# Splitting the SSD layer's weights by transfers: a cast on the way in, and a second, accumulating transfer for the remainder

## The chip, the cores and the metric

The kernel runs on one core of one Trainium2 chip. The metric is the device time of one execution in microseconds, given as the median of several runs. The profile and the trace come from one more execution of the same program.

## The reference, cut to what matters

One inference step through two layers, in float32: a Mamba-2 SSD mixer and then a gated MLP with position mixing, each behind an RMS norm and added to the residual. 640 tokens (512 of a new stream, 8 times 16 of running streams) of width 1024 go through. The change touches the weights of the first layer's two projections:

```python
def mamba2_mixer(h, conv_prev, ssm_prev, w_in, conv_w, conv_b, dt_bias, a_log, d_skip, norm_w, w_out):
    proj = h @ w_in
    z = proj[..., :D_INNER]
    xbc = proj[..., D_INNER:D_INNER + CONV_DIM]
    dt_raw = proj[..., D_INNER + CONV_DIM:]
    xbc_c, conv_new = causal_dwconv(xbc, conv_prev, conv_w, conv_b)
    xbc_c = jax.nn.silu(xbc_c)
    ...
    y, ssm_new = ssd_scan(xs, dt, a, bm, cm, ssm_prev)
    y = y + d_skip.astype(jnp.float32)[:, None] * xs.astype(jnp.float32)
    y = gated_group_rms_norm(y.reshape(bsz, seq_len, D_INNER), z, norm_w).astype(h.dtype)
    return y @ w_out, conv_new, ssm_new.astype(ssm_prev.dtype)
```

## The kernel before

Matrix products run on values in the type float32r, which keeps fewer bits than float32. To hold the accuracy, each operand is split into a high part H (the value rounded to float32r) and a low part L (what is missing), and a product is three matmuls: H by H, H by L and L by H. Activations are split when they are made. The weights come from memory as float32 tiles of 128 x 1024 (512 KB) and are split on the core.

The split of the first layer's weights is `wsplit` (L93). SP issues the transfer into a tile `raw` (L95; two buffers), ScalarE copies it into `wh` with the rounding (L99), and VectorE or POOL subtracts: `wl` = `raw` - `wh` (L100). Both `wh` and `wl` have four buffers. `Stream` (L106) keeps the list of tiles in order of use; `next` hands out the next tile and first calls `wsplit` for tiles up to two beyond it (`Stream(units, 2)`, L318). `on_pool` (L317) names the tiles whose subtraction is on POOL: tiles 3 to 6, all tiles z0 and all tiles of the output projection; the others are on VectorE. The very first tile goes another way (`first`, L116) and isn't touched by the change.

The work goes by eight groups of four heads. For a group, the input projection is made of six tiles, x0, x1, B, C, z0 and z1 (those of x0 and x1 of the second group are done within the first; 48 matmuls each in `in_proj`, L258), and from the second group on two tiles "o" of the output projection of the group before. PE's order in a group is: x0, x1, B, C, z0, then scan, output projection of the group before (ten pieces of 512 columns, `out_proj`, L270) and the pair products mixed, then z1. After the last group of this layer the stream's list goes on into tiles of the second layer; what is loaded ahead of these is not used.

Behind each projection of x0, x1, B and C stands a convolution, `conv_tile` (L406). POOL clears and fills the first columns of `xp`, VectorE moves the PSUM result into it, POOL copies the last columns out, ScalarE does the first tap and VectorE the other three, and then ScalarE a tanh:

```python
            G.memset(xp[:, 0:3], 0.0)
            G.tensor_copy(out=xps[:, :, 0:3], in_=cch[:, j])
            V.tensor_tensor(out=xp[:, 3:387], in0=o0, in1=rb[:, 0:384], op=ALU.mult)
            ...
            G.tensor_copy(out=nconv[:, j, 0, :], in_=xp[:, 512:515])
            G.tensor_copy(out=nconv[:, j, 1:9, :], in_=xps[:, :, 16:19])
            ...
            S.activation(acc[:, 0:664], xp[:, 0:664], AF.Identity, scale=cw[:, 4 * ft:4 * ft + 1],
                         bias=cw[:, 128 + ft:129 + ft])
            for k in range(1, 4):
                V.scalar_tensor_tensor(acc[:, 0:664], xp[:, k:k + 664], cw[:, 4 * ft + k:4 * ft + k + 1], acc[:, 0:664],
```

Its result `xc` (L428, L429) is transposed by PE (`to_tokens`, L465) in the middle of the next projections, and from the transposed x VectorE makes `xdt` (L479) and POOL `xw` (L481). Other work of POOL in a group: eight products that decay the old states (`h`, L587) and one mask of `E` (L631). `E` are tiles of decays, read by SP from a table in device memory (`laD`, L513), one per head, and worked on by ScalarE (L515, L516).

PE's instructions run in the order of the code. In this layer the order on the other engines is made when the kernel is built, by a scheduler that places instructions by their estimated times and by what they wait for; every engine then works its list in that order, and an instruction that waits holds up those behind it. DMA issues stand in the list of the engine that issues them. In the second layer all orders are those of the code. Of the first layer's norm, the sum of squares (L185 to L189) and the projection of dt (`dtT`, L182) matter below.

Of the kernel before, what the change touches and what calls it, by code (L numbers as in the profile page):

```python
# [8 lines left out]
F32 = mybir.dt.float32  # L9
F32R = mybir.dt.float32r  # L10
I32 = mybir.dt.int32
AF = mybir.ActivationFunctionType
ALU = mybir.AluOpType
PSUM = bass.MemoryType.PSUM

P = 128
# [24 lines left out]
def hybrid_step(ctx: ExitStack, tc: tile.TileContext, xin, xT0, cst, wdt, cache, wA, wAo, h0in, wB, wBv, wBo,  # L41
                lnwb, spc, bsp, nwb, y_out, nconv_out, sspP_out, sspS_out, v_out):
    nc = tc.nc
    V, S, G, T = nc.vector, nc.scalar, nc.gpsimd, nc.tensor
# [3 lines left out]
    wpool = ctx.enter_context(tc.tile_pool(name="wpool", bufs=3))  # L48
# [13 lines left out]
    def C(n):  # L62
        a, b = _C[n]
        return csb[0][:, a:b] if b <= NCST1 else csb[1][:, a - NCST1:b - NCST1]
# [25 lines left out]
        return r  # L90


    def wsplit(eng, pool, src, scale=None):  # L93
        raw = (pool or wpool).tile([P, 1024], F32, name="raw", tag="raw", bufs=2)
        nc.sync.dma_start(out=raw, in_=src)  # L95
        H = wpool.tile([P, 1024], F32R, name="wh", tag="wh", bufs=4)
        L = wpool.tile([P, 1024], F32R, name="wl", tag="wl", bufs=4)
        if scale is None:
            S.copy(out=H, in_=raw)  # L99
            eng.tensor_tensor(out=L, in0=raw, in1=H.bitcast(F32), op=ALU.subtract)  # L100
        else:
            S.activation(H, raw, AF.Identity, scale=scale)
            V.scalar_tensor_tensor(L, raw, scale, H.bitcast(F32), ALU.mult, ALU.subtract)
        return H, L

    class Stream:  # L106
        def __init__(self, srcs, ahead):
            self.srcs, self.ahead, self.got, self.n, self.pools = srcs, ahead, [], 0, {}

        def fill(self, ahead):  # L110
            while len(self.got) < min(len(self.srcs), self.n + ahead):
                i = len(self.got)
                self.got.append(wsplit(G if i in on_pool else V, self.pools.get(i), *self.srcs[i]))


        def first(self, n, between):  # L116
# [141 lines left out]
    def in_proj(W, xT, pool=None, tag="in", at=(1, 3, 5, 7, 9, 11, 13)):  # L258
        outs = []
        for h, (a, b) in enumerate(HALVES):  # L260
            o = (pool or ps_in).tile([P, 512], F32, name="pin", tag=tag)[:, :b - a]
            outs.append(o)
            for k in range(KD):
                in_proj_step(W, xT, o, h, k)
                if 8 * h + k in at:
                    pump()
        return outs
# [36 lines left out]
    units, names = [], []  # L304
# [9 lines left out]
        units += [p[1:] for p in part]  # L314
    units += wo(GROUPS - 2) + wo(GROUPS - 1)
    units += [(wBv[i],) for i in range(16)]
    on_pool = {3, 4, 5, 6} | {i for i, n in enumerate(names) if n in ("z0","o")}  # L317
    stream = Stream(units, 2)  # L318


    with ExitStack() as ca:
# [35 lines left out]
        for d in (15, 13, 11, 9, 7, 5, 3):  # L357
# [17 lines left out]
                        in1=C("blk").rearrange("p (b o) -> p b o", o=1).broadcast_to([P, 8, HEADS]), op=ALU.mult)  # L375
# [69 lines left out]
        for g in range(GROUPS):  # L445
# [77 lines left out]
            if g:  # L523
                queue(0, *(() if g == 1 else (0,)))
                o = in_proj(stream.next(), xT, ps_m, "m", at=(3, 7, 11, 14))
                xcs.append(conv_tile(*o, 16 + g, 2, *cio))
                queue(1, *(() if g == 1 else (1,)))
                o = in_proj(stream.next(), xT, at=(3, 7, 11, 14))
# [683 lines left out]
```

## Time and profile before

| | us |
|---|---|
| median of 3 runs | 1113.79 |
| lowest, highest | 1112.61, 1121.4 |
| the profiled execution | 1111.67 |
| its span, first to last instruction | 1109.9 |

| engine | busy us | share of the span |
|---|---|---|
| PE (matmuls) | 1035.4 | 93% |
| PEld (weight loads, beside the matmuls) | 931.0 | 84% |
| DVE (VectorE) | 903.4 | 81% |
| ACT (ScalarE) | 442.6 | 40% |
| POOL (GpSimd) | 204.2 | 18% |

The first layer takes the first 620 us or so of the span. "Busy" counts the time in which an engine has at least one instruction at work. A releaser is what an idle engine waited for last. The time from a transfer's issue to its landing is shown with the tile that it fills.

### The profile page before, as it was taken

The page shows a single profiled execution, that of the slowest core. Times are in us where ns is not written, and L with a number is a line of the kernel's source. Part 1 is how long each engine was busy: PE and PEld are TensorE (multiplying, and loading weights), DVE is VectorE, ACT ScalarE, POOL GpSimd, SP SyncE. Part 2 cuts the span into 40 slices and gives each one's busy share as a digit, 9 for nine tenths or more (in the row PEclk, how much of TensorE's full clock was granted, in tenths as well). Part 3 has the DMA queues.
Part 4 walks back from the last instruction along what each step waited for, and adds up shares of the span by engine and source line. Part 5 has one row for each costly group of instructions (what it writes and reads, how often), then busy time and mean ns, then how long its engine had stood idle before and what let it go on. Part 6 is the DMA issues. An engine that isn't in the chain of part 4 may idle for free.

```text
span 1109.9 us, 16925 instructions
## 1 busy us (share of the span) xinstructions
PE 1035.4 (93%) x6387; PEld 931.0 (84%) x6387; DVE 903.4 (81%) x1575; ACT 442.6 (40%) x803; POOL 204.2 (18%) x303
## 2 busy tenths in 40 slices
PE   8898999898999998989999899987999999999996
PEld 7797888798898897987997688877898988988985
DVE  7869887979878888798789866667888888888876
ACT  6363516235163262452532443354433432423343
POOL 3434323404224043042141000000000000000000
PEclk9898999999999999999999899999999999999998
DMA  7453534253363442623533322202322412413222
GB/s 252 137 181 102 166 114 162 88 177 98 93 207 100 122 144 86 208 71 103 202 94 126 131 72 80 84 22 78 95 81 65 131 59 81 135 50 90 89 67 94
DMA packets 57216, 125.93 MB, mean 113 GB/s; under 512 B 9104, under 2 KB 27792, under 8 KB 57136
## 3 DMA queue, kind: packets, MB, share of 16 engines
q1 hardware_dynamic: 57136, 124.87, 35.5%
q8 instruction: 50, 0.82, 0.3%
q14 instruction: 30, 0.25, 0.1%
HBM read 107.98 MB, written 16.86 MB: 112 GB/s over the span
## 4 chain that ended last, share of the span: by engine, by line
PE 42%; DVE 36%; ACT 10%; DMA 6%; issue 4%; SPq 0%; POOL 0%; ACTq 0%; DVEq 0%
PE pop L69 11%; PE pin L69 9%; PE pv L69 7%; DVE acc L422 7%; DMA E<-laD 5%; DVE wf L749 4%; PE pqb L69 3%; PE pqc L69 2%; PE pqa L69 2%; ACT E L515 2%; DVE h L965 2%; DVE E L631 2%; PE st L69 2%; PE yB L69 1%; ACT wf L748 1%
## 5 line engine op out<-in xcount | busy, mean ns | idle before, releaser
L69 PE MATMUL pin<-xH,wh 128*128 128x384 f32 (+1 forms) x768 | 249.1, 324 | 10.9 <-DVE xp L412 10.2
L69 PE MATMUL pin<-xH,wl 128*128 128x384 f32 (+1 forms) x768 | 239.1, 311 | 0.5 <-DVE wl L100 0.5
L69 PE MATMUL pin<-xL,wh 128*128 128x384 f32 (+1 forms) x768 | 238.8, 311 | 0.0
L69 PEld LDWEIGHTS pin<-xH,wh 128*128 128x128 f32 x768 | 146.8, 191 | 19.0 <-ACT xc L428 11.3
L69 PEld LDWEIGHTS pin<-xL,wh 128*128 128x128 f32 x768 | 147.3, 192 | 0.4 <-issue 0.3
L69 PEld LDWEIGHTS pin<-xH,wl 128*128 128x128 f32 x768 | 146.9, 191 | 0.8 <-DVE wl L100 0.8
L422 DVE SCALAR_TENSOR_TENSOR acc<-xp,cw,acc 128x664 f32<-128x664 f32 x96 | 115.8, 1206 | 19.2 <-ACT acc L419 17.9
L69 PE MATMUL pop<-wf,yHL 128*128 128x512 f32 x480 | 116.4, 398 | 8.7 <-DVE h L965 8.0
L69 PEld LDWEIGHTS pop<-wf,yHL 128*128 128x128 f32 x480 | 88.8, 188 | 34.2 <-DVE h L965 12.8
L99 ACT CAST wh<-raw 128x1024 fp32r<-128x1024 f32 x65 | 67.6, 1042 | 102.9 <-PE pin L69 62.6
L749 DVE TENSOR_TENSOR wf<-raw,wf 128x512 fp32r<-128x512 f32 x128 | 88.0, 692 | 25.1 <-ACT wf L748 22.7
L69 PE MATMUL pop<-wh,yHL 128*128 128x512 f32 x320 | 103.5, 405 | 5.2 <-DVE hs L566 4.4
L748 ACT CAST wf<-raw 128x512 fp32r<-128x512 f32 x128 | 76.5, 615 | 78.8 <-PE pop L69 28.8
L69 PEld LDWEIGHTS pop<-wh,yHL 128*128 128x128 f32 x320 | 57.7, 188 | 20.9 <-DVE hs L566 6.7
L686 DVE SCALAR_TENSOR_TENSOR h<-pop,rr,h 128x512 f32<-128x512 f32 x80 | 58.8, 742 | 12.0 <-PE pop L69 11.9
L69 PE MATMUL pqa<-xH,wf 128*128 128x320 f32 x256 | 63.6, 317 | 5.3 <-ACT v L841 3.2
L69 PE MATMUL pqb<-tf,wf 128*128 128x320 f32 x384 | 63.0, 313 | 2.0 <-DVE zz L1027 2.0
L69 PE MATMUL pv<-wh,xL 128*128 128x512 f32 x160 | 63.4, 396 | 1.0 <-DVE xL L231 1.0
L69 PE MATMUL pv<-wh,xH 128*128 128x512 f32 x160 | 63.7, 398 | 0.0
L69 PE MATMUL pv<-wl,xH 128*128 128x512 f32 x160 | 63.3, 395 | 0.0
L69 PE MATMUL pop<-wl,yHL 128*128 128x512 f32 x160 | 62.6, 391 | 0.0
L862 POOL MEMSET spt<- 64x64 f32 x8 | 1.2, 146 | 320.6 <-DMA spt<-spc 184.4
(221 smaller groups left out, 2072.5 us busy)
## 6 DMA issues: line engine op xcount, KB each, us to landing
raw<-wA SPq DMA_DIRECT2D x47, 512.0 KB, 3.8
raw<-wB SPq DMA_DIRECT2D x32, 512.0 KB, 3.8
E<-laD SPq DMA_DIRECT2D x32, 320.0 KB, 6.8
raw<-wBv SPq DMA_DIRECT2D x18, 512.0 KB, 3.8
h<-h0in SPq DMA_DIRECT2D x16, 512.0 KB, 4.7
raw<-wAo SPq DMA_DIRECT2D x16, 512.0 KB, 4.1
out_sspS<-h SPq DMA_DIRECT2D x16, 512.0 KB, 3.7
raw<-wBo SPq DMA_DIRECT2D x16, 512.0 KB, 3.7
```

The costliest lines, as they stand in the source:

```text
L69: T.matmul(out, lhsT=lhsT, rhs=rhs, start=start, stop=stop, **kw)
L99: S.copy(out=H, in_=raw)
L422: V.scalar_tensor_tensor(acc[:, 0:664], xp[:, k:k + 664], cw[:, 4 * ft + k:4 * ft + k + 1], acc[:, 0:664], ALU.mult, ALU.add)
L515: S.activation(E_[:, t, :], E_[:, t, :], AF.Relu, bias=la[:, t, h:h + 1], scale=-1.0)
L631: (G if i and (last or e) else V).tensor_tensor(out=Es[2 * i + e], in0=Es[2 * i + e], in1=CBm, op=ALU.mult)
L686: V.scalar_tensor_tensor(h1[:, t, dsl], ps, rg[:, t:t + 1], h1[:, t, dsl], ALU.mult, ALU.add)
L748: S.copy(out=t[:, 0], in_=src)
L749: V.tensor_tensor(out=t[:, 1], in0=src, in1=t[:, 0].bitcast(F32), op=ALU.subtract)
L862: G.memset(spt[64:128, 0, 0:64], 0.0)
L965: V.scalar_tensor_tensor(h1[:, t, dsl], ps, 0.5, h1[:, t, dsl], ALU.mult, ALU.add)
```

## The change

`wsplit` has no `raw` tile, no subtraction and no choice of engine any more. POOL issues a transfer from the float32 weights into the float32r tile `wh` (the cast transfer, L97 of the changed kernel). ScalarE writes the negated `wh` into `wl` (L98). POOL then issues a second transfer of the same weights, which adds them to what stands in `wl` (the accumulating transfer, L99). `next` calls `wsplit` for tiles up to three beyond the one it hands out, where it was two.

```diff
-    def wsplit(eng, pool, src, scale=None):
-        raw = (pool or wpool).tile([P, 1024], F32, name="raw", tag="raw", bufs=2)
-        nc.sync.dma_start(out=raw, in_=src)
+
+    def wsplit(src):
         H = wpool.tile([P, 1024], F32R, name="wh", tag="wh", bufs=4)
         L = wpool.tile([P, 1024], F32R, name="wl", tag="wl", bufs=4)
-        if scale is None:
-            S.copy(out=H, in_=raw)
-            eng.tensor_tensor(out=L, in0=raw, in1=H.bitcast(F32), op=ALU.subtract)
-        else:
-            S.activation(H, raw, AF.Identity, scale=scale)
-            V.scalar_tensor_tensor(L, raw, scale, H.bitcast(F32), ALU.mult, ALU.subtract)
+        G.dma_start(out=H, in_=src)
+        S.activation(L, H.bitcast(F32), AF.Identity, scale=-1.0)
+        G.dma_start(out=L, in_=src, accum_op=ALU.add)
         return H, L
...
-                self.got.append(wsplit(G if i in on_pool else V, self.pools.get(i), *self.srcs[i]))
+                self.got.append(wsplit(*self.srcs[i]))
...
-    on_pool = {3, 4, 5, 6} | {i for i, n in enumerate(names) if n in ("z0","o")}
-    stream = Stream(units, 2)
+    stream = Stream(units, 3)
```

PE's order is the same but for the numbers of some tiles. The lines of the changed kernel behind the diff carry numbers that are 5 lower: L405 there is L410 here. Three places of the new orders follow.

POOL, from the end of one group's second stretch on, in the kernel before: the subtraction L100 for two tiles, the memset and copy into `xp` (L410, L411), the copies out (L416, L417) and `xw` (L481).

```order
L100 TENSOR_TENSOR wl<-raw,wh 128x1024
L410 MEMSET xp 128x3
L411 COPY xp<-cch 128x8x3
L416 COPY nconv<-xp 128x3
L417 COPY nconv<-xp 128x24
L100 TENSOR_TENSOR wl<-raw,wh 128x1024
L481 TENSOR_TENSOR xw<-xdt,esu 128x4x128
L410 MEMSET xp 128x3
L411 COPY xp<-cch 128x8x3
L481 TENSOR_TENSOR xw<-xdt,esu 128x128
```

The same place on POOL in the changed kernel, where L97 is the cast and L99 the accumulating transfer:

```order
L97 DMA wh<-wA 128x1024
L411 COPY nconv<-xp 128x3
L412 COPY nconv<-xp 128x24
L405 MEMSET xp 128x3
L406 COPY xp<-cch 128x8x3
L99 DMA wl<-wA 128x1024
L97 DMA wh<-wAo 128x1024
L411 COPY nconv<-xp 128x3
L412 COPY nconv<-xp 128x24
L476 TENSOR_TENSOR xw<-xdt,esu 128x4x128
L99 DMA wl<-wAo 128x1024
L476 TENSOR_TENSOR xw<-xdt,esu 128x128
```

Cast and accumulating transfers take turns, tile by tile, with POOL's other work between and behind them; each L99 waits for ScalarE's negation of the tile just cast.

ScalarE at the start of a group in the kernel before: the cast from `raw` (L99), the convolution's first tap (L419) and tanh (L428), and the work on `E`.

```order
L99 CAST wh<-raw 128x1024
L419 ACTIVATE acc<-xp,cw 128x664
L516 ACTIVATE E<-E 128x640
L515 ACTIVATE E<-E,la 128x128 x6
L516 ACTIVATE E<-E 128x640
L515 ACTIVATE E<-E,la 128x128
L428 ACTIVATE xc<-acc 128x512
L428 ACTIVATE xc<-acc 128x128
L515 ACTIVATE E<-E,la 128x128 x4
L99 CAST wh<-raw 128x1024
L419 ACTIVATE acc<-xp,cw 128x664
```

The same place in the changed kernel; L98 is the negation, L414 the first tap, L423 the tanh:

```order
L98 ACTIVATE wl<-wh 128x1024
L675 ACTIVATE y<-y 128x640
L510 ACTIVATE E<-E,la 128x128 x5
L511 ACTIVATE E<-E 128x640
L414 ACTIVATE acc<-xp,cw 128x664
L510 ACTIVATE E<-E,la 128x128 x6
L511 ACTIVATE E<-E 128x640
L98 ACTIVATE wl<-wh 128x1024
L423 ACTIVATE xc<-acc 128x512
L423 ACTIVATE xc<-acc 128x128
```

The weight instruction stood behind the first tile's tanh and now stands ahead of it.

POOL at the start of the program in the kernel before, with the sums of squares on L188:

```order
L410 MEMSET xp 128x3 x2
L188 ISA
L188 TENSOR_TENSOR sqa_125<-sqa_125,xt 128x640 x3
L411 COPY xp<-cch 128x8x3 x2
L100 TENSOR_TENSOR wl<-raw,wh 128x1024 x2
```

And in the changed kernel, where they are on L184:

```order
L405 MEMSET xp 128x3 x2
L97 DMA wh<-wA 128x1024 x3
L99 DMA wl<-wA 128x1024
L184 ISA
L184 TENSOR_TENSOR sqa_125<-sqa_125,xt 128x640
L99 DMA wl<-wA 128x1024
L184 TENSOR_TENSOR sqa_125<-sqa_125,xt 128x640
L99 DMA wl<-wA 128x1024
L184 TENSOR_TENSOR sqa_125<-sqa_125,xt 128x640
L97 DMA wh<-wA 128x1024
```

Three cast transfers are issued at once, and each sum stands behind an accumulating transfer.

## Rows read from the trace of the kernel before

**Rows 1.** The page's part 1: busy us, share of the span, instructions, by engine.

```profile
PE 1035.4 (93%) x6387; PEld 931.0 (84%) x6387; DVE 903.4 (81%) x1575; ACT 442.6 (40%) x803; POOL 204.2 (18%) x303
```

**Rows 2.** Windows: us, busy PE, PEld, DVE, ACT, POOL, clock, DMA share, GB/s: stretches x0-z0.

```profile
313.60:353.70 40.10, 37.53 (x263) 36.51 (x262) 34.42 (x61) 23.52 (x49) 14.63 (x23) 1.00 0.48 150
...
sum 246.50, PE 228.83 PEld 222.41 DVE 206.62 ACT 141.94 POOL 84.03; mean PE 38.14 PEld 37.07 DVE 34.44 ACT 23.66 POOL 14.00
```

**Rows 3.** The same by window: five stretches between those; the start.

```profile
sum 161.90, PE 157.45 PEld 131.63 DVE 137.87 ACT 29.92 POOL 32.50; mean PE 31.49 PEld 26.33 DVE 27.57 ACT 5.98 POOL 6.50
...
0.00:165.90 165.90, 150.04 (x987) 136.81 (x988) 136.99 (x238) 74.84 (x142) 58.02 (x76) 0.96 0.49 159
```

**Rows 4.** Chain of waits, 313 to 347 us: start, us, what.

```profile
313.57 5.04 DMA E<-laD
...
322.66 2.32 DVE acc L422
...
330.34 2.35 DVE rt L85
...
339.80 2.26 DVE acc L422
```

**Rows 5.** Timeline, 329 to 331 us, DVE and POOL: start, us, what.

```profile
330.14 0.17 DVE L84 TENSOR_TENSOR rt<-rr 128x5 f32<-128x5 f32 x1
330.34 2.34 DVE L85 SCALAR_TENSOR_TENSOR rt<-rt,rx 128x5 f32<-128x5 f32 x1
...
330.26 2.40 POOL L100 TENSOR_TENSOR wl<-raw,wh 128x1024 fp32r<-128x1024 f32 x1 [0.37 <-ACT wh L99]
```

**Rows 6.** Tile acc, first 620 us: ns min/median/max, first and last start.

```profile
L422 DVE SCALAR_TENSOR_TENSOR acc<-xp,cw,acc x96: 894/909/2994, 39.7 to 568.8; 128x664 f32<-128x664 f32 x96
```

**Rows 7.** Groups by line, first 620 us: busy us, mean ns | idle before, releasers.

```profile
L99 ACT CAST wh<-raw 128x1024 fp32r<-128x1024 f32 x65 | 67.6, 1042 | 102.9 <-PE pin L69 62.6 <-PE pop L69 34.0 <-DMA raw<-wA 6.3
L100 POOL TENSOR_TENSOR wl<-raw,wh 128x1024 fp32r<-128x1024 f32 x23 | 55.9, 2432 | 13.5 <-ACT wh L99 13.5
L100 DVE TENSOR_TENSOR wl<-raw,wh 128x1024 fp32r<-128x1024 f32 x42 | 52.6, 1252 | 7.1 <-ACT wh L99 7.0
```

**Rows 8.** Tiles raw, then E: issues on SP in ns; landing in us.

```profile
L95 SPq DMA_DIRECT2D raw<-wA x47: 327/334/1452, 8.2 to 537.1; - x47
...
DMA to landing us min/median/max: 3.3/3.8/7.7
...
DMA to landing us min/median/max: 4.1/6.8/9.5
```

**Rows 9.** Timeline, POOL, the long form of xw.

```profile
334.38 1.65 POOL L481 TENSOR_TENSOR xw<-xdt,esu 128x512 f32<-128x512 f32 x1 [1.72 <-DVE xdt L479]
```

**Rows 10.** Windows of 4 us: columns as in rows 2.

```profile
316.00:320.00 4.00, 4.00 (x32) 4.00 (x31) 2.77 (x5) 2.19 (x5) 0.00 (x0) 1.00 0.98 337
```

**Rows 11.** Timeline, ScalarE: tanh of x0.

```profile
327.24 0.83 ACT L428 ACTIVATE xc<-acc 128x512 f32<-128x512 f32 x2 [0.58 <-DVE acc L422]
```

**Rows 12.** Timeline, PE: first matmuls of x0 and x1, transposes, a gap.

```profile
313.12 0.34 PE L69 MATMUL pin<-xH,wh 128*128 128x384 f32 x1
...
320.16 0.34 PE L69 MATMUL pin<-xH,wh 128*128 128x384 f32 x1
...
329.87 0.60 PE L469 MATMUL tp<-csb,xc 128*128 128x128 f32 x4
...
345.90 0.41 PE L69 MATMUL pin<-xH,wh 128*128 128x384 f32 x1 [1.93 <-DVE xp L412]
```

**Rows 13.** Timeline of the start: ScalarE, POOL, DVE.

```profile
19.43 0.72 ACT L182 COPY dtT<-pin 64x384 f32<-64x384 f32 x2
...
18.46 1.73 POOL L188 TENSOR_TENSOR sqa<-sqa,xt 128x640 f32<-128x640 f32 x1 [0.39 <-ACT xt L187]
...
22.86 0.82 DVE L189 TENSOR_TENSOR sqa<-sqa,sqa 128x640 f32<-128x640 f32 x1
```

**Rows 14.** Transfers, first 620 us: packets, MB, share of 16 engines.

```profile
q1 hardware_dynamic: 37199, 86.04, 43.4%
```

More of the change, by code (lines that the diff above doesn't have):

```diff
@@ L107, in __init__ @@
         def __init__(self, srcs, ahead):
-            self.srcs, self.ahead, self.got, self.n, self.pools = srcs, ahead, [], 0, {}
+            self.srcs, self.ahead, self.got, self.n = srcs, ahead, [], 0
         def fill(self, ahead):
```

## The prediction

> **What bounds the kernel now.** I read the page's busy shares first: PE has work in 93% of the span and DVE in 81%, POOL in 18% [rows 1]. PE is near its end, DVE close behind. The change touches only the first 620 us (the SSD layer), so I cut that part by what PE does. From the third group of heads on, each group has two stretches. In the first, five input projections run back to back (x0, x1, B, C, z0): six such stretches take 246.5 us, of which PE is busy 228.83, so 17.7 us are idle, 2.9 us each [rows 2]. In the second, the output projection and z1 run: five of them leave PE idle for 161.9 - 157.45 = 4.5 us, under 1 us each [rows 3]. The first 165.9 us (start, first two groups) leave 15.9 us idle [rows 3]. So whatever VectorE gains, about 18 us can come from the six stretches, and a few more from the start.
>
> What holds PE in a stretch is read from the chain of waits [rows 4]: a transfer of E, the ScalarE work behind it, then for 23 us VectorE with hardly a break, until PE starts again at 345.90 after 1.93 us of idle. Three of these VectorE steps take 2.3 us, and the timeline shows why for one of them: a tile of 128x5 elements, 0.17 us otherwise, takes 2.34 us while POOL does one of the subtractions of wsplit, 2.40 us [rows 5]. The other two are convolution steps on L422, whose median is 0.91 us and whose longest takes 2.99 [rows 6].
>
> **What goes.** wsplit's subtraction leaves both engines: 42 on DVE, 52.6 us, and 23 on POOL, 55.9 us [rows 7], and with these the stalls just shown. In a stretch VectorE is busy 34.4 of 40.1 us [rows 2]. It loses about two subtractions of its own (2.5 us) and, with POOL's three, three stalls of 1.4 to 2.2 us (2.3 less 0.9 or 0.17): some 8 us. It then needs 26 us for 40 and isn't the bound; the 2.9 us of idle would go. I take them in full, 6 x 2.9 = 17.7 us, since the waits named in a stretch are VectorE's or hang on its xc.
>
> **What comes.** ScalarE keeps one instruction per tile: the negation for the cast, 1024 elements each, 1.04 us [rows 7]. Nothing on balance. SP loses its 65 issues, POOL gets two for each of 66 tiles (one more is loaded ahead). Neither a cast nor an accumulating transfer, nor any transfer issued by POOL, stands in the trace, so their cost has to be bounded.
>
> The order on POOL is what matters. A tile is now cast transfer, wait, accumulating transfer, and POOL's next cast transfer stands behind that wait: POOL handles nearly one tile at a time. Before, a transfer of one tile waited for nothing of another but its raw buffer. So each tile has a loop: issue of the accumulating transfer of the tile before, issue and landing of the cast, ScalarE's turn, negation.
> - Issue: on SP one takes 0.33 us [rows 8]. POOL may have to do more; its nearest row of work of its own, one step of the xw product, takes 1.65 [rows 9]. These are my bounds; I take the middle, 1.0.
> - Landing, from issue: 3.8 us median for these tiles, 3.3 to 7.7; E's take 6.8 [rows 8]. With 0.67 more for the issue I take 4.5 as a base. The cast follows an accumulating transfer of the same size on the same queue, issued 1.0 us earlier. At the 337 GB/s of a window with the engines 98% busy [rows 10], 512 KB take 1.56 us; reading source and old contents makes that 3.1, so the cast waits 2.1 us for it at most, 0 at least. I take 1.05: landing 5.5.
> - ScalarE: 1.05 us, and half of one such instruction, 0.5, until it is free.
>
> The loop is 1.0 + 5.5 + 0.5 + 1.05 = 8.05 us; with all lower bounds 0.33 + 3.8 + 1.04 = 5.2, with no queueing 7.0, with the full 2.1 us 9.1, and 10 to 12 if landings go to the upper end of their row.
>
> One of the Trainium skill's rules would make it shorter. It gives transfers issued by POOL as about 2.0 us plus bytes over 436 GB/s (DMA: Bandwidth & Descriptors, "Anatomy of one DMA — SWDGE (gpsimd) path"), 3.2 us for 512 KB. No row of before shows a transfer by POOL; the row of SP's has 3.8. With 3.2 in place of 5.5 the loop would be 5.75 us, less than PE takes for a projection, and the outcome would be that of the fast rival below. Against it, another of its rules says that an engine consumes descriptors in ring order (same page, "Queues, rings and completion order"); by that the cast does stand behind the accumulating transfer, as I assume.
>
> PE's projection takes 7.05 us without a gap (313.12 to 320.16, [rows 12]). Buffers come free one per projection, so in a stretch five loads come at PE's pace and the loop must keep up. The weights themselves aren't late: a buffer freed at 320.16 is needed three projections on, 21 us later, and loop plus a second landing are some 14. What is late is what stands behind the wait. ScalarE's new order puts the negation ahead of the tanh of the convolution (xc, L428), which in before ran at 327.24 [rows 11], and PE transposes that result at 329.87 [rows 12]. Count from the buffer's release at 320.16: landing 5.5, ScalarE 0.5 and 1.05, tanh 0.83, VectorE's xc 0.9 make 328.9: 0.9 us to spare on the first tile. Each further tile is 8.05 - 7.05 = 1.0 us later, and POOL's memset and copy into xp, and the xw product, stand behind the accumulating transfer too. So a stretch changes by 5 x (8.05 - 7.05) - 2.9 = +2.1 us; six make +12.6. The second stretches have two loads in 24 us of output projection and don't change.
>
> At the start POOL has an accumulating transfer ahead of the third sum of squares; that waits for a negation which ScalarE's order puts behind the copies of dtT (19.43 + 0.72 us). 20.15 + 1.05 + 1.0 = 22.2 for a sum that began at 18.46, 1.73 us, and whose result was added at 22.86 [rows 13]: 22.2 + 1.73 = 23.9, 1.1 us late, and up to 3 if the first casts take bandwidth from xt. I take +2. VectorE's relief in the first 165.9 us could give some of its 15.9 us back; the bounds are 0 and 8, and I take 0, since this part also has its loads one after another.
>
> **The sum.** +12.6 + 2 = +14.6 us on a span of 1109.9 us (execution 1111.67). The median of the runs lies 2.1 us higher, at 1113.79: I predict 1128 us.
>
> **The rivals.**
> - *The loop keeps up* (under 7.05 us; no queueing, or transfers by POOL as quick as the skill's fit). Then the six stretches give 17.7 us and the start costs 2: 1098, at best 1090 with the start's 8 us. For it: 3.8 us is the median of SP's transfers, and the loop with no queueing is 7.0. Against it: from 316 to 320 us the DMA engines are 98% busy [rows 10], with the transfers of E (6.8 us, [rows 8]) just where a stretch begins, and accumulating transfers come on top. Chance 0.25.
> - *Both cancel* (loop 7.05 to 7.7 us): 6 x (5 x 0.35 - 2.9) + 2 = -5 at its middle, 1109. Chance 0.16.
> - *The DMA engines become the bound.* They are 43.4% busy over the 620 us [rows 14]; a stretch is at 0.48 of 40.1 us [rows 2], 19.2 us, of which five loads are 7.8. If an accumulating transfer takes three times a plain one (4.7 us), five tiles need 31 us, with the rest 42.5, more than the stretch. E's transfers then land up to three such, 14 us, later; less the 2.9 us, 6 x 11.1 + 2 gives 1182. Nothing in the trace speaks for the factor three, nothing against it. Chance 0.12.
> - *The change doesn't do what it says*: a subtraction left on VectorE. Its new order has none, so no chance.
>
> **Chances and range.** The likeliest case, a loop of 7.7 to 9.2 us, has 0.47 and runs by the same formula from 1118 to 1163. A run of this kernel can be told from no change at about 1% (1102.7 to 1124.9). Faster: the first rival and a little of the second, 0.27. Same: the rest of the second and the lower end of the likeliest, 0.23. Slower: 0.50. The range of 8 in 10 goes from 1094 (the fast rival but for its best part) to 1170.
>
> **What would show it.** POOL's rows of both transfers: their duration, near 1.0 us; the median landing of the cast, near 5.5, and of the accumulating transfer. In a stretch: a time from one cast's issue to the next of 8 us, not 7; waits of ScalarE on the wh transfer and of PE or its weight load on xc, where VectorE's accumulations now take 0.9 us and VectorE is busy about 26 us in 40. The prediction is wrong if casts land within 4.5 us of their release (then PE's idle in a stretch goes below 1 us), or if the accumulating transfers fill the DMA engines (share over 0.9 in the stretches, and PE waiting for wl itself).

## The result, and the profile after

The change makes the kernel slower: 1181.72 us median (1178.22 to 1188.45) against 1115.88 in runs taken beside it, ratio 1.0592, 95% interval [1.0526, 1.0658], or 66 us. The direction was predicted; 1128 us was far too little, and 1182 lies above the range's 1170. The profiled execution took 1181.53 us, its span 1179.4, 69.5 more than before's.

I cut both traces at the same places of the program, at TensorE's first matmul of x0 and last of z0 in each group from the third on. First the kernel before, cut this way, a little wider than in [rows 2, 3]: six first stretches, then five second ones (windows; columns as in rows 2).

```profile
sum 247.66, PE 229.99 PEld 223.67 DVE 206.67 ACT 143.58 POOL 84.03; mean PE 38.33 PEld 37.28 DVE 34.45 ACT 23.93 POOL 14.00
...
sum 158.96, PE 154.51 PEld 128.69 DVE 136.43 ACT 27.39 POOL 32.50; mean PE 30.90 PEld 25.74 DVE 27.29 ACT 5.48 POOL 6.50
```

The same views of the changed kernel, with one stretch of each kind ahead of its sum:

```profile
332.23:377.82 45.59, 39.60 (x266) 38.47 (x265) 26.85 (x54) 22.29 (x44) 12.82 (x29) 0.96 0.70 192
...
sum 271.68, PE 237.66 PEld 229.62 DVE 160.85 ACT 132.28 POOL 76.54; mean PE 39.61 PEld 38.27 DVE 26.81 ACT 22.05 POOL 12.76
...
377.82:416.21 38.39, 32.84 (x207) 27.08 (x206) 24.95 (x44) 7.62 (x12) 11.70 (x16) 0.96 0.58 127
...
sum 185.93, PE 160.85 PEld 132.17 DVE 125.66 ACT 39.23 POOL 58.18; mean PE 32.17 PEld 26.43 DVE 25.13 ACT 7.85 POOL 11.64
```

So the 69.5 us are: first stretches +24.0, second stretches +27.0, the rest of the program from the last z0 on (572.2 to the end, now 625.8 to the end) +16.0, the start +2.6. VectorE did fall to 26.8 us in a stretch, but TensorE's idle time in the first stretches went from 17.7 to 34.0 us. Its busy time grew too, by 7.7 and 6.3 us, with the same matmuls: the granted clock reads 0.96 or less in eight of the eleven stretches, where before it was 1.00 in all but one.

The waits of the first 690 us (who waited for whom: us, times, longest), for POOL, ScalarE, VectorE and TensorE:

```profile
POOL wl L99 <- ACT wl L98: 204.9, 58, 11.8
POOL wh L97 <- PE pop L69: 87.3, 8, 14.2
...
ACT wl L98 <- DMA wh<-wA: 102.2, 32, 9.1
...
DVE CBm L591 <- DMA dhl<-hl: 25.4, 6, 5.6
...
PE tp L464 <- DVE xc L424: 33.9, 14, 4.9
```

The first and third are the loop that the prediction describes, and the last is where it reaches TensorE: these waits for xc lie in the first stretches and are all but 0.1 of the 34.0 us of idle time there. The wait for dhl was not foreseen. POOL's timeline of one first stretch has the casts' issues, and the chain of waits has one turn of the loop:

```profile
332.63 0.55 POOL L97 DMA_DIRECT2D wh<-wA  x1 [3.85 <-PE pin L69]
...
341.47 0.82 POOL L97 DMA_DIRECT2D wh<-wA  x1
...
352.90 0.87 POOL L97 DMA_DIRECT2D wh<-wAo  x1
...
362.29 0.61 POOL L97 DMA_DIRECT2D wh<-wAo  x1
...
371.88 0.61 POOL L97 DMA_DIRECT2D wh<-wA  x1
...
379.49 0.89 POOL L97 DMA_DIRECT2D wh<-wA  x1
```

```profile
352.90 6.34 DMA wh<-wAo
...
359.31 1.07 ACT wl L98
360.38 0.42 issue
360.80 0.89 POOL wl L99
361.70 0.44 POOL xw L476
...
362.29 6.54 DMA wh<-wAo
```

Five turns take 46.9 us, 9.4 each (7.6 to 11.4; the mean over all six stretches is 9.4 too), where 8.05 was predicted and TensorE needs 7.05 for a projection alone.

Behind a first stretch the chain shows a second mechanism. hl holds the samples' xw and B; SP sends it to DRAM as dhl, and it shares its one buffer with CBm, so VectorE may not write CBm until that transfer has landed. ScalarE's negation stands ahead of a tanh, that ahead of VectorE's xc, and behind xc in VectorE's order stands the last piece of hl (L487):

```profile
295.15 1.06 ACT wl L98
296.21 0.53 ACT xc L423
...
296.76 0.89 DVE xc L424 x2
297.66 0.07 DVE hl L487
...
297.89 6.75 DMA dhl<-hl
...
304.73 0.48 DVE CBm L591
...
309.46 2.93 PE pop L69 x6
```

### The profile page after: what moved, and what is told of

It reads as the page before. It is cut to its first block, busy times and chain, and to the rows that moved or that the text cites. A ratio compares the mean times of both kernels' runs of the same rounds, so it can differ in the third digit from the quotient of the medians.

```text
span 1179.4 us, 16944 instructions
## 1 busy us (share of the span) xinstructions
PE 1053.0 (89%) x6387; PEld 945.2 (80%) x6387; DVE 826.2 (70%) x1533; ACT 447.1 (38%) x804; POOL 228.2 (19%) x412
## 4 chain that ended last, share of the span: by engine, by line
PE 29%; DVE 22%; DMA 19%; issue 16%; ACT 8%; POOL 5%; SPq 0%; POOLq 0%; ACTq 0%; DVEq 0%
PE pv L69 9%; DMA wh<-wAo 7%; PE pop L69 6%; PE pin L69 5%; DMA wh<-wA 4%; DVE wf L744 4%; DMA dhl<-hl 3%; PE pqb L69 2%; DMA E<-laD 2%; ACT wl L98 2%; PE pqc L69 2%; DMA out_sspS<-h 2%; POOL wl L99 2%; DVE h L960 2%; PE pqa L69 1%
## 5 line engine op out<-in xcount | busy, mean ns | idle before, releaser
L69 PE MATMUL pin<-xH,wh 128*128 128x384 f32 (+1 forms) x768 | 252.5, 329 | 0.1
L69 PE MATMUL pin<-xL,wh 128*128 128x384 f32 (+1 forms) x768 | 241.8, 315 | 0.0
L69 PE MATMUL pin<-xH,wl 128*128 128x384 f32 (+1 forms) x768 | 241.7, 315 | 0.0
L69 PEld LDWEIGHTS pin<-xH,wh 128*128 128x128 f32 x768 | 149.8, 195 | 7.9 <-issue 4.3
L69 PEld LDWEIGHTS pin<-xL,wh 128*128 128x128 f32 x768 | 149.9, 195 | 0.2
L98 ACT ACTIVATE wl<-wh 128x1024 fp32r<-128x1024 f32 x66 | 69.9, 1059 | 192.0 <-DMA wh<-wA 102.2
L417 DVE SCALAR_TENSOR_TENSOR acc<-xp,cw,acc 128x664 f32<-128x664 f32 x96 | 91.9, 957 | 35.1 <-ACT acc L414 33.5
L424 DVE SCALAR_TENSOR_TENSOR xc<-xc,acc 128x512 f32<-128x512 f32 x64 | 35.5, 594 | 59.4 <-ACT xc L423 59.3
L99 POOL DMA_DIRECT2D wl<-wA x47 | 41.3, 878 | 176.6 <-ACT wl L98 151.5
```

The source lines that it names most:

```text
L69: T.matmul(out, lhsT=lhsT, rhs=rhs, start=start, stop=stop, **kw)
L98: S.activation(L, H.bitcast(F32), AF.Identity, scale=-1.0)
L99: G.dma_start(out=L, in_=src, accum_op=ALU.add)
L424: V.scalar_tensor_tensor(o, o, 1.0, a, ALU.add, ALU.mult)
```

## The experiments

All times are medians, each compared with the kernel before as run on the same chip (1115.4 to 1116.2 us). The table at the end of the section has every run by the four parts of the program.

**Loop or load.** The negation and the accumulating transfer of a tile (wlow) come one tile later, just ahead of the next cast (wcast).

```diff
-self.got.append(wsplit(*self.srcs[i]))
+self.got[i - 1] = wlow(self.got[i - 1], *self.srcs[i - 1])
+self.got.append(wcast(*self.srcs[i]))
```

> Two theories on the 66 us that the change costs. T1, the waits in the orders: POOL's accumulating transfer waits for ScalarE's negation, that for the cast's landing, and all that stands behind on POOL and ScalarE waits too. T2, the load: two transfers of 512 KB for each tile, one of them accumulating, make every transfer land later. This kernel is the changed one with the same transfers, negations and sizes, but with the negation and the accumulating transfer of a tile issued one tile later, just ahead of the next cast, so that the cast has had a projection's time (7 us) to land. T1: ScalarE's wait for the cast, 148 us in the changed kernel, falls below 40 us, the six first stretches go from 48 us back to 42 or less, and the time is 1140 us or lower. T2: the landings stay at 6.5 us, the stretches above 46 us, and the time is over 1165 us.

1176.52 us, ratio 1.0546 [1.0516, 1.0577]. ScalarE still waited 154 us for casts and POOL 204 us for negations. The time lies in T2's range, but this decides nothing: in POOL's order each cast still stands behind the accumulating transfer of the cast before it, so the loop was whole. It was moved, not cut.

**A plain second transfer.**

```diff
-G.dma_start(out=L, in_=src, accum_op=ALU.add)
+G.dma_start(out=L, in_=src)
```

> The changed kernel with the second transfer plain instead of accumulating (the low parts are then the weights themselves: this part of the computation is changed); every instruction and its order stay. T1 (waits in the orders): the loop of cast, negation and second transfer stays, so 1165 to 1182 us. T2 (load, with the accumulation as its dear part): the DMA engines' time on the weights falls by a third or more, the landing of the casts goes from 6.6 towards 4.5 us, and the time is 1145 us or lower.

1130.06 us, 1.0116 [1.0095, 1.0138]: 52 of the 66 us hang on the accumulation. In this kernel casts land in 5.0 us median instead of 6.1 (each follows the second transfer of the tile before on one queue), and POOL's second issue takes 0.53 us instead of 0.88. The first stretches lose 26 us. By the forecast the time speaks for T2, but what changed fits a shorter loop and a lighter load alike.

**The load alone.**

```diff
 nc.sync.dma_start(out=raw, in_=src)
+twin = twins[0].tile([P, 1024], F32, name="twin", tag="twin", bufs=2)
+nc.sync.dma_start(out=twin, in_=src)
```

> The kernel before, with every weight tile from the third on loaded a second time by SP into a tile that nobody reads: the load of the changed kernel without an accumulation and without a wait. T1: landings get later, by 1 to 2 us, but the weights are loaded early enough, 1113 to 1125 us. T2: the transfers of E and of the samples' stack land as late as in the changed kernel (dhl 6.9 us instead of 2.4), and the time is 1135 us or more.

1121.22 us, 1.0041 [1.0025, 1.0058], first stretches 251.2 us, second ones unchanged. Twice the weight traffic from SP's queue costs 5 us, and dhl lands in 3.4 us. T2 as a mere load falls.

**The cast alone.**

```diff
-S.copy(out=H, in_=raw)
+G.dma_start(out=H, in_=src)
```

> One half of the change alone: the high parts come by a cast transfer of POOL, the tile is also loaded as before by SP, and the low parts are subtracted as before on VectorE and POOL; no accumulating transfer, no instruction of ScalarE. T1: POOL's transfers wait only for a free buffer, so the loop is gone: 1105 to 1130 us. T2: two loads of each tile as in the changed kernel, one of them plain: 1140 us or more.

1162.78 us, 1.0423 [1.0398, 1.0448]: in T2's range and a miss for T1 as I had put it. POOL waits 136 + 93 us at the cast's issue, for TensorE to free a wh buffer, and 23 subtractions and the xw products stand behind that; SP in turn waits 134 us for POOL's subtractions before it may load raw again. A wait for a free buffer, harmless on SP, blocks POOL's work.

**The loop cut.** A scheduler sets POOL's order, and it would put the accumulating transfer first again. So both of these kernels hold POOL to the order of the program text. From the third group on, the orders of all engines are the same but for the tile that negation and accumulating transfer handle and one VectorE step on hl in each group.

```diff
+ca.enter_context(tc.manual_schedule(engines={mybir.EngineType.Pool}))
```

> The changed kernel with POOL's instructions of the SSD layer held in the order of the program text, as a control for the next run; in the six first stretches POOL's order is cast, accumulating transfer of the same tile, then the rest, as in the changed kernel. All theories: 1170 to 1190 us.

```diff
-self.got.append(wsplit(*self.srcs[i]))
+self.got.append(wcast(*self.srcs[len(self.got)]))
+self.low(len(self.got) - 2)
```

> The control with one difference: the accumulating transfer (and its negation) in each place is that of the tile cast before, not of the tile cast just ahead of it. The transfers, their number and their order by kind stay; a cast now has a whole projection to land before POOL waits for it. L, the loop: cast, landing, negation and accumulating transfer, one tile at a time, take over 8 us against the 7.05 us of a projection; that the plain second transfer gave back 51 us comes from a loop shorter by 1.6 us, 5 x 6 times. By L ScalarE's wait for casts falls below 50 us, the first stretches from 48 to 43 us or less, and the time is 1145 us or lower. A, the accumulations themselves: they hold the DMA engines so long that the other transfers land late whatever POOL's order is: landings stay as late, the time is 1160 us or more.

1278.09 us, 1.1437 [1.1394, 1.1480], and 1205.92 us, 1.0815 [1.0772, 1.0858]. The control missed by 90 us: in text order POOL's mask products of a pair stand behind casts that wait for the output projection to free its buffers (TensorE waits 63 us for them), and second stretches take 47 us. But the two differ in little else than that one tile, and the first stretches don't have those masks. The control's windows of these, then POOL's wait from the third group on:

```profile
sum 282.91, PE 240.36 PEld 230.15 DVE 174.94 ACT 137.03 POOL 78.10; mean PE 40.06 PEld 38.36 DVE 29.16 ACT 22.84 POOL 13.02
```

```profile
POOL wl L98 <- ACT wl L97: 270.4, 44, 9.9
```

With the loop cut:

```profile
sum 254.81, PE 231.23 PEld 221.26 DVE 154.52 ACT 129.46 POOL 83.80; mean PE 38.54 PEld 36.88 DVE 25.75 ACT 21.58 POOL 13.97
```

```profile
POOL wl L98 <- ACT wl L97: 15.1, 9, 2.3
```

POOL's wait goes from 270 to 15 us and the first stretches lose 28.1 us, though accumulations and transfers are all still there and E lands later (8.8 us, 7.0 in the control). So the loop costs 28.1 / 30 = 0.94 us for each tile in this pair: 19.0 us are idle time of TensorE (0.63 a tile), and 9.1 are its busy time, at a granted clock of 0.93 to 1.00 in the control and 1.00 without the loop. The forecast's other signs of L missed: ScalarE's wait for casts is 113 us there, not under 50, and the time, with a control 90 us off, is far above 1145.

**No cast, no loop.** SP loads, ScalarE rounds and negates, POOL only accumulates; then the same without accum_op, and without the last line.

```diff
-G.dma_start(out=H, in_=src)
+nc.sync.dma_start(out=raw, in_=src)
+S.copy(out=H, in_=raw)
 S.activation(L, H.bitcast(F32), AF.Identity, scale=-1.0)
 G.dma_start(out=L, in_=src, accum_op=ALU.add)
```

> The other half of the change alone: the tile comes by SP into a buffer and ScalarE rounds it into the high parts, as before; ScalarE negates them and POOL's accumulating transfer adds the tile a second time. No cast transfer. L (loop): SP fetches two tiles ahead, so nothing goes round in a loop, POOL waits for ScalarE alone: 1110 to 1140 us. A (accumulations): they are all still there: 1155 us or more.

> The kernel without a loop (SP loads, ScalarE rounds and negates, POOL's second transfer) with that second transfer plain instead of accumulating; every instruction and wait stays in its place (the low parts are then the weights themselves). With the accumulation its six first stretches took 251.2 us, without any second transfer 229.8. If the 21 us are the accumulations' time in the DMA engines (by the queue's busy time 3.1 us for one, 1.75 for a plain one, and E's transfers behind them): stretches of 230 to 238 us, 1110 to 1120 us in all. If they are POOL's instructions behind its wait for ScalarE's negation: 246 us or more, over 1128 us.

> What the relief of VectorE alone can give. SP loads the tile and ScalarE rounds it, as in the kernel before; ScalarE writes the negated high parts, and nothing is added to them (the low parts are left out of the computation): no subtraction, no transfer by POOL, one load for each tile. The prediction's gain: without the subtractions the 17.7 us of idle time in the six first stretches go: these fall from 247.7 to about 231 us, and the time to about 1095 us. Rival: VectorE isn't what ends the wait last, ScalarE's work on E after its transfer is: the first stretches stay above 243 us, the time above 1106 us. Against the kernel with the same work and the accumulating transfer (1136 us) the difference is what 66 such transfers cost without a loop.

1136.07 us, 1.0181 [1.0146, 1.0216]; 1116.60 us, 1.0003 [0.9988, 1.0019]; 1084.55 us, 0.9721 [0.9694, 0.9747]. The first lies in L's range. The last shows the predicted gain in full:

```profile
sum 229.82, PE 227.37 PEld 222.55 DVE 164.73 ACT 171.80 POOL 38.99; mean PE 37.89 PEld 37.09 DVE 27.46 ACT 28.63 POOL 6.50
```

17.8 us less than before in the first stretches, and 9 more at the start. Against it 66 accumulating transfers without a loop cost 51.5 us, and 66 plain ones 32. In the first stretches 21.4 us come with the accumulations, of which making them plain gives back only 7.0; the forecast for that run had 13 or more, or under 5, and neither came. How the other 14 divide between one more load (3.5 us in the run that loaded twice, less than one profile varies by) and POOL's work behind its wait for ScalarE stays open.

From these kernels, one profile each, the first stretches of the changed one add up within rounding: 247.7, less 17.8 for the relief, with 21.4 for the accumulating transfers without a loop and 20.5 for the casts on POOL, which close the loop, make 271.7.

**hl in a buffer of its own**, and then also without the three tiles of wBv that the stream loads at its end and nobody uses.

```diff
-hl = wk.tile([P, 2, 384], F32R, name="hl", tag="CBm", bufs=1)
+hl = wk.tile([P, 2, 384], F32R, name="hl", tag="hl", bufs=1)
```

> The changed kernel with one tile, hl, in a buffer of its own instead of CBm's, the order of all instructions unchanged. In the changed kernel VectorE waits 25 us in all for the transfer of hl to land before it may write CBm, and the second stretches are 12 us longer than before. If this wait is what makes them longer: 1168 to 1175 us, second stretches back to 32 to 33 us. If the wait lies beside another (the loop or the clock), less than 4 us change: 1178 us or more.

```diff
-units += [(wBv[i],) for i in range(16)]
```

> The last kernel with hl in a buffer of its own, and without the tiles of wBv at the end of the stream's list: three of them are loaded, cast, negated and accumulated there though the next layer loads its own. In the kernel with hl's own buffer the time from the last z0 to the end of the program was 551.4 us, against 537.7 before the change. If these tiles are what the border between the layers costs: 538 to 541 us, so 1141 to 1146 us in all. If the border waits for something else: over 1150 us.

> The kernel before, without the tiles of wBv at the end of the stream's list (two are loaded and split there without use). If they cost the border what they take on VectorE and ScalarE, 2 x 1.25 us and some of the transfers: 1110 to 1114 us; if they lie beside other work, 1114 to 1117 us.

1155.05 us, 1.0332 [1.0290, 1.0375], with the order of all instructions unchanged. The second stretches by windows:

```profile
sum 158.51, PE 154.61 PEld 128.65 DVE 125.72 ACT 39.03 POOL 58.35; mean PE 30.92 PEld 25.73 DVE 25.14 ACT 7.81 POOL 11.67
```

All 27 us of them are gone, clock included: the shared buffer was their whole cost. (My forecast had 12 us, since I had cut the stretches at VectorE's steps, which were late themselves.) Without the unused tiles 1140.82 us, 1.0238 [1.0179, 1.0297]; the rest of the program is 539.1 us against 551.4. So these tiles were most of the border's 16.0: there TensorE waits 14.4 us in one piece in the changed kernel, 1.6 without them and 3.8 in the kernel before. In the kernel before two such tiles cost nothing that can be measured: 1114.05 us, 0.9987 [0.9967, 1.0006].

**Where the gain comes from, and a better kernel.** Before's 23 POOL tiles (three at the start, eight of z0 and twelve of the output projection, whose last four are on VectorE) by ScalarE's negation and an accumulating transfer, the others untouched; the same for the 20 tiles of z0 and the output projection alone, with the two edits above; and before with all subtractions on VectorE.

```diff
-eng.tensor_tensor(out=L, in0=raw, in1=H.bitcast(F32), op=ALU.subtract)
+if eng is G:
+    S.activation(L, H.bitcast(F32), AF.Identity, scale=-1.0)
+    G.dma_start(out=L, in_=src, accum_op=ALU.add)
+else:
+    eng.tensor_tensor(out=L, in0=raw, in1=H.bitcast(F32), op=ALU.subtract)
```

> One edit of the kernel before: for the 23 tiles whose subtraction POOL did, ScalarE negates the high parts and POOL's transfer adds the tile, behind SP's load and ScalarE's rounding as they were. hl's buffer and the unused tiles stay as before. If the gain of 27 us of the mixture is POOL's subtractions that are gone: first stretches 226 to 230 us, 1088 to 1094 us. If it needed hl's own buffer or the tiles at the end: 1100 us or more.

> A mixture that could be better than both: the kernel before, with the accumulating transfer (behind SP's load, ScalarE's rounding and its negation) for those tiles alone whose subtraction POOL did, z0 and the output projection; four tiles at the start go from POOL to VectorE, hl has its own buffer, and the unused tiles at the end are gone. POOL's subtractions and VectorE's stalls of 1.4 to 2.2 us beside them go; 19 accumulating transfers come. If the stalls were what idles TensorE in the first stretches and the accumulations don't hold anything up: 1095 to 1108 us. If an accumulation holds POOL's order up behind ScalarE as in the kernel with 66 of them (23 us slower): 1115 to 1125 us.

```diff
-on_pool = {3, 4, 5, 6} | {i for i, n in enumerate(names) if n in ("z0","o")}
+on_pool = set()
```

> The kernel before with all 65 subtractions on VectorE, POOL has none. If POOL's subtractions cost VectorE its stalls (1.4 to 2.2 us beside each) more than a subtraction of 1.25 us would: 1095 to 1110 us, first stretches below 243 us. If VectorE's own work is what bounds the stretches: 34.4 of 41 us plus 3 x 1.25 less the stalls, no gain, 1113 to 1125 us.

1089.06 us, 0.9763 [0.9738, 0.9788]; 1088.85 us, 0.9758 [0.9733, 0.9784]; 1091.79 us, 0.9789 [0.9764, 0.9814]. All three beat both kernels, the first and the last by one edit each; the last two came out below their forecasts. The first stretches by windows, first with 23 accumulating transfers, then with all subtractions on VectorE:

```profile
sum 226.46, PE 226.10 PEld 222.32 DVE 181.83 ACT 157.88 POOL 52.22; mean PE 37.68 PEld 37.05 DVE 30.31 ACT 26.31 POOL 8.70
```

```profile
sum 227.40, PE 226.51 PEld 222.39 DVE 196.44 ACT 143.41 POOL 52.49; mean PE 37.75 PEld 37.07 DVE 32.74 ACT 23.90 POOL 8.75
```

TensorE has 0.4 and 0.9 us of idle time left there. That POOL's list holds other work up less is not the reason: with the accumulating transfers POOL waits 45 us for ScalarE's negations from the third group on, where it waited 5 us for ScalarE's rounding before. With POOL's subtractions added to its own VectorE is busy 196.4 us there instead of 206.7, since its stalls beside these subtractions are gone. The longest convolution step (tile acc, ns min/median/max), 2994 ns in [rows 6], is now:

```profile
L422 DVE SCALAR_TENSOR_TENSOR acc<-xp,cw,acc x96: 898/907/1583, 39.3 to 547.9; 128x664 f32<-128x664 f32 x96
```

All runs, from one profile each, in us (in one profile the first stretches vary by some 6 with the granted clock, as the third row shows, whose change touches only the border):

| kernel | start, to x0 of the third group | six first | five second | rest | span |
|---|---|---|---|---|---|
| before | 165.6 | 247.7 | 159.0 | 537.7 | 1109.9 |
| changed | 168.2 | 271.7 | 185.9 | 553.6 | 1179.4 |
| before, no unused tiles | 167.2 | 253.8 | 158.9 | 536.3 | 1116.2 |
| low part one tile later | 170.3 | 272.2 | 182.6 | 548.3 | 1173.4 |
| plain second transfer | 167.2 | 245.5 | 172.4 | 543.9 | 1128.9 |
| before, loaded twice | 171.8 | 251.2 | 158.9 | 538.0 | 1119.9 |
| cast alone | 180.8 | 263.3 | 179.1 | 542.8 | 1165.9 |
| POOL in text order | 204.4 | 282.9 | 236.0 | 556.6 | 1279.9 |
| the same, loop cut | 177.5 | 254.8 | 218.8 | 553.4 | 1204.5 |
| no cast, accumulating | 175.5 | 251.2 | 161.9 | 544.3 | 1132.8 |
| no cast, plain | 168.6 | 244.2 | 160.2 | 540.4 | 1113.4 |
| no cast, no second transfer | 156.5 | 229.8 | 158.1 | 536.9 | 1081.3 |
| hl's own buffer | 169.1 | 274.6 | 158.5 | 551.4 | 1153.5 |
| the same, no unused tiles | 163.8 | 277.1 | 158.2 | 539.1 | 1138.2 |
| 23 accumulating, one edit | 163.2 | 226.5 | 158.9 | 538.6 | 1087.2 |
| 20 accumulating, two edits more | 166.4 | 226.3 | 159.0 | 535.4 | 1087.1 |
| all on VectorE | 164.9 | 227.4 | 158.9 | 538.3 | 1089.5 |

## Why the prediction was wrong in size

- **VectorE's relief, 17.7 us: held.** With neither subtraction nor second transfer the first stretches lose 17.8 us. It is POOL's subtractions that held VectorE up, not VectorE's own 42: leaving those in place loses nothing (226.5 us with them, 229.8 without). The prediction took the whole relief as one term and so did not see that moving 23 tiles would do.
- **The loop, 5 x (8.05 - 7.05) a stretch: the mechanism held, the sum did not.** TensorE idles where the prediction said, waiting for xc behind the negation (33.9 us). But a turn took 9.4 us, and with that the formula gives 5 x (9.4 - 7.05), nearly 12 us of idle time a stretch, where 5.7 came. Its pace is too short as well: a stretch has 38.3 us of TensorE's work, 7.7 for each of five tiles and not 7.05. So it is luck that the formula's 5.0 lies near 5.7, and the 0.94 us a tile of the pair above, in another order of POOL and with the clock in it, doesn't confirm the 1.0. By its pieces: the issue 0.88 us (1.0 taken), the landing 6.1 median (5.5 taken), the negation 1.06 (1.05), and a hand-over of 0.42 from ScalarE to POOL and POOL's own steps, which had no term. Of 55 casts issued right behind an accumulating transfer, 45 had it still under way and landed in 6.8 us median, the other ten in 3.9: the queueing, taken as 1.05 and at most 2.1, was 2.9. The rows of both transfers, from the tiles wh and wl: issue in ns, then landing in us, wh's first.

```profile
L97 POOL DMA_DIRECT2D wh<-wA x47: 535/602/952, 1.3 to 600.7; - x47
...
DMA to landing us min/median/max: 3.8/6.1/10.7
...
L99 POOL DMA_DIRECT2D wl<-wA x47: 847/878/955, 14.9 to 609.8; - x47
...
DMA to landing us min/median/max: 5.2/6.0/11.3
```

- **The first stretches, +2.1 us each: mis-sized, +4.0.** Loop and gain net gave 12.6 us; 24.0 came. Against the relief alone that is 41.9 us where the loop had 30, and 21.4 of them are there with the accumulating transfers alone, without cast and loop: the prediction put that cost at nothing. 1.3 us a stretch are more busy time at a lower granted clock, a term that was missing too.
- **"The second stretches have two loads in 24 us of output projection and don't change": the step that failed most.** It cost 27.0 of the 55 us that the sum fell short by. I counted the loads there and didn't ask which other transfer a VectorE step waits for. The transfer of hl lands in 6.9 us median where it took 2.4 (the issues of both kernels below, before first; the last number is the median us to landing), and its issue is late, in the third group 3.8 us after z0's end (217.3 and 213.5 us), before 1.8 ahead of it. The prediction named the negation ahead of the tanh, but followed it only to TensorE's transposes, not to hl, its buffer and CBm.

```profile
dhl<-hl SPq DMA_DIRECT2D x8, 384.0 KB, 2.4
```

```profile
dhl<-hl SPq DMA_DIRECT2D x8, 384.0 KB, 6.9
```

- **"One more is loaded ahead": seen and costed at nothing.** Three unused tiles at the border of the layers were 12 of the 16.0 us there.
- **The start, +2: the number came, +2.6, in part by luck.** The sums of squares were added at 27.52 us instead of 22.86, 4.7 us late and not 1.1; TensorE waited 2.0 us for them, and 2.9 for xH where it had been 0.8. VectorE's relief there was taken as 0, but the kernel with the relief alone is 9 us faster at the start; as far as that holds here too, the costs were as much above 2.
- **The rivals.** The loop that keeps up fell, and so did the fit behind it: the Trainium skill's 3.2 us for 512 KB by POOL (DMA: Bandwidth & Descriptors, "Anatomy of one DMA — SWDGE (gpsimd) path") lies below each landing seen, 3.8 us at best for a cast in the changed kernel (3.6 in any kernel here), 5.2 for an accumulation. The Trainium skill's rule of ring order (same page, "Queues, rings and completion order") agrees with the trace as far as seen: each of the 45 casts landed after the accumulating transfer that was still under way ahead of it. "The DMA engines become the bound" gave 1182 us and so the measured time, by another way: the engines are busy for 0.70 of a stretch, not over 0.9, and an accumulation takes them about 3.2 us, not 4.7. Its number came out by chance, but the doubled time (3.1 us) that I had used for the queueing was near. Neither of the prediction's two signs of being wrong came: casts landed in 6.1 us median, not within 4.5, and the share stayed under 0.9. Half of the error lay in the second stretches, for which it had no sign.

## What to carry to other kernels

An instruction that waits for another engine, put on an in-order queue that also issues transfers, turns independent loads into a loop; compare the loop's length with the consumer's pace, and follow everything behind it to the last buffer that it shares. When a transfer becomes slower or later, list the buffers with two uses whose second writer waits for its landing, for that wait may stand in a stretch that the change doesn't touch. Where the trace shows stalls of one engine beside another's work, try first to take away just that work: here 24 of the 27 us to be had came from emptying one list.

## What the runs showed of the hardware

- An accumulating transfer of 512 KB keeps the 16 DMA engines busy for about 3.2 us, a cast for 1.73. The first is worked out from 23 of them (queue, packets, MB, share of 590 us), the second from 65 casts alone (share of 690 us):

```profile
q0 software_dynamic: 3312, 12.06, 12.4%
```

```profile
q0 software_dynamic: 9360, 34.08, 16.3%
```

- POOL issues an accumulating transfer in 0.88 us, a plain one or a cast in 0.53 to 0.60; SP's issues take 0.33 [rows 8].
- Idle time of TensorE can cost twice. In the control with POOL in text order it idles 13 us of each second stretch and its mean granted clock is 0.86 there, between the two levels of 1.2 and 2.4 GHz; the same matmuls then take 171.4 us instead of 154.5. The sum of idle time alone doesn't settle it: of the changed kernel's second stretches, two with 5.3 and 5.5 us of it read 1.00, three with 4.0 to 5.6 read 0.95 or 0.96.
- One subtraction of 128x1024 takes 2.43 us on POOL [rows 7] and 1.25 us on VectorE, and VectorE's steps beside POOL's stretch: each of the 14 steps of L422 above 2 us (0.91 median, 2.99 at most, [rows 6]) ran beside one. Moving 23 subtractions to VectorE made the kernel 24 us faster.
